# The last norm of a hybrid convolution layer: means taken from two places, powers without a Newton step, a spread in quarters

## The chip, the cores and the metric

The kernel runs on one NeuronCore of a Trainium2 chip. The metric is the device time of one execution in microseconds (us); smaller is better. A core has a matrix engine (TensorE, PE in the profile), a vector engine (VectorE, DVE), a scalar engine (ScalarE, ACT), a general engine (GpSimd, POOL) and a queue engine (SyncE, SP). Each works through its own instructions in order, and they wait for one another by semaphores. Transfers between HBM and the on-chip memory SBUF are issued here from SP and from ACT. PSUM is the memory into which TensorE writes; VectorE and ScalarE can read it.

## The reference, cut to what matters

One layer: a short gated convolution, then a SwiGLU feed-forward part, each between two RMS norms, with shift, scale and gate from a conditioning vector. There are 2048 tokens of 1024 features, in float32.

```python
def rms_norm(x, g):
    xf = x.astype(jnp.float32)
    y = xf * lax.rsqrt(jnp.mean(xf * xf, axis=-1, keepdims=True) + RMS_EPS)
    return (y * g.astype(jnp.float32)).astype(x.dtype)

mod = c_act @ ada_w[i] + ada_b[i]
sh_m, sc_m, g_m, sh_f, sc_f, g_f = jnp.split(mod, N_ADA, axis=-1)
h = modulate(rms_norm(x, norm_gains[i, 0]), sh_m, sc_m)
h = short_conv_mixer(h, conv_w_in[j], conv_w[j], conv_w_out[j])
x = x + g_m[:, None, :] * rms_norm(h, norm_gains[i, 1])
h = modulate(rms_norm(x, norm_gains[i, 2]), sh_f, sc_f)
h = swiglu(h, ffn_w_gate_up[i], ffn_w_down[i])
x = x + g_f[:, None, :] * rms_norm(h, norm_gains[i, 3])
```

The last line is what the end of the kernel computes for its last 512 tokens.

## The kernel before

**Tiles and stages.** Features lie on the 128 partitions and tokens along the free axis, in tiles of 128 x 512, so that a vector of 1024 features is eight tiles (`KD = 8`). The tokens are worked in two halves of 1024 (`NU = 2`), and each of these in two groups of 512 (`tok` 0 and 1). Four matrix products follow one another for each half: `in`, `out`, `gu` and `down`; the stages run in the order in0, out0, in1, out1, gu0, down0, gu1, down1. Each product is worked with seven products of blocks instead of eight (P1 to P7), and each of these with operands split into a high and a low part in a shorter float format (three passes in place of a float32 one).

**The order of the work.** The program is written out by hand, slot by slot. A slot is one product of blocks on TensorE. `later(n, f)` puts a step `n` slots behind the present one, and `due()` runs what has come due, once ahead of a slot's product and once behind it (the half slots). All engines take their instructions in the order in which the program is written.

**A norm.** The squares of eight tiles are added up in one tile (`add_square`: the square by ACT, the add by GpSimd, or by VectorE for some tiles of the last stage). `norm_of_sums` takes the mean over the partitions: for each 128 tokens, a product with the sum's columns as stationary operand and a column of 1/1024, so that 128 means lie in one column of a PSUM bank. `root` (line 218) raises mean + eps to the power -1/2 on GpSimd, and then does a Newton step in three operations on VectorE, whose result is the power times -2; line 158 multiplies the gains by -0.5 to make up for it. `diagonal` puts the four columns of 128 factors on the diagonals of four 128 x 128 blocks, and `spread` multiplies them by a matrix of ones, so that each of the 512 tokens has its factor on all partitions. `root` is used in sixteen places: twice in the start (lines 1111 and 1260, names r0 and r1), for the rows of the second half (r2, r3), behind each `out` stage (n.., m..), behind each `down` stage (o..), and in `last_half`.

**The start.** `vt` holds the small vectors (biases, gains, taps, conditioning), loaded by ACT's queue. VectorE sets some constants, waits for `vt` to scale the gains (line 158), and then fills `w` with ones (line 1200), with which `warm(8)` runs passes on TensorE that compute nothing used. The first factor is worked from the squares of the rows in `factor(0)`, spread, and multiplied into the first features.

**The last stage.** In down1 the slots are sorted so that the tiles of the second token group become ready one after another (line 511). The tiles are `down1z`; when one is ready, `ready_z` (line 649) has its square taken and added (`down1q`), and the tile scaled by gain and gate on ACT. The eighth has a square of its own (`ph.sq`, in the profile `lastq`). Then `last_half` (line 1011) runs:

- for five tiles (`ON_PE`), x times the identity is put into a PSUM bank (`lastx`) ahead of time, two before the means and three behind them;
- the means of the sum of seven squares and of the eighth square, eight products of one column each for both (`lasts`);
- eps and the sum of the two (`lastv`), power (`lastp`), Newton step (`lastt`, and `lastq` again), diagonal (`lastd`), spread (`lastb`, one product over 512 columns);
- for each tile, VectorE multiplies z by the spread in PSUM. For the five of `ON_PE` TensorE adds z to x in `lastx`, ACT copies the bank and issues the output; for the other three VectorE adds x and SP issues the output.

A float32 product takes two passes on TensorE in the profile. Every operation is recorded on line 78, that of the helper `Engine`, so the profile's rows are told apart by the names of tiles.

Of the kernel before, what the change touches and what calls it, by code (L numbers as in the profile page):

```python
# [10 lines left out]
F32 = mybir.dt.float32  # L11
F32R = mybir.dt.float32r
AF = mybir.ActivationFunctionType
ALU = mybir.AluOpType

P = 128
# [3 lines left out]
KD = D // P  # L20
NF = FF // P
FH = NF // 2
EPS = 1e-6
CH = 512
# [13 lines left out]
VB, VG, VW, VC = 0, 48, 80, 104  # L38
# [11 lines left out]
def hybrid_conv_layer(  # L50
# [31 lines left out]
    V, A, PE, G, SP = map(Engine, (nc.vector, nc.scalar, nc.tensor, nc.gpsimd, nc.sync))  # L82
# [4 lines left out]
    bigs, pairs, raws, sb = (ctx.enter_context(tc.tile_pool(name=n, bufs=1)) for n in ("bigs", "pairs", "raws", "sb"))  # L87
# [12 lines left out]
    def tmp(name):  # L100
        return sb.tile([P, CH + 2], F32, tag="tmp", bufs=NTMP, name=name)

    def small(n, name):
        return sb.tile([P, n], F32, tag="small", bufs=16, name=name)

    def bank(name):
        return ps.tile([P, CH], F32, tag="mm", bufs=8, name=name)
# [5 lines left out]
    def later(slots, f):  # L113
        waiting.append((now[0] + slots, len(waiting), f))
# [26 lines left out]
    vt = const.tile([P, 112 + 24], F32, name="vt")[:, :112]  # L141
    A.dma_start(vt, vec)
    ident = const.tile([P, P], F32, name="ident")
# [4 lines left out]
    one = const.tile([P, P], F32, name="one")  # L148
    V.memset(one, 1.0)
    mean = const.tile([P, 1], F32, name="mean")  # L150
    V.memset(mean, 1.0 / D)
    mhalf = const.tile([P, 4], F32, name="mhalf")
# [2 lines left out]
    V.memset(carry, 0.0)  # L155
    cact = const.tile([P, KD], F32, name="cact")
    A.activation(cact, vt[:, VC : VC + KD], AF.Silu)
    V.tensor_scalar(vt[:, VG : VG + 4 * KD], vt[:, VG : VG + 4 * KD], -0.5, None, ALU.mult)
    mA = [const.tile([P, KD], F32, name=f"mA{i}") for i in range(2)]
    mB = [const.tile([P, KD], F32, name=f"mB{i}") for i in range(2)]  # L160
    mG = [const.tile([P, KD], F32, name=f"mG{i}") for i in range(2)]
# [1 line left out]
    def col(t, k):  # L163
        return t[:, k : k + 1]
# [52 lines left out]

    def root(v, name):

        p, t = small(4, name + "p"), small(4, name + "t")  # L220
        G.tensor_tensor(p, v, mhalf, ALU.pow)
        yield 1
        q = sb.tile([P, 4], F32, tag="q", bufs=8, name=name + "q")
        V.tensor_tensor(t, p, p, ALU.mult)
        V.tensor_tensor(t, t, v, ALU.mult)
        V.scalar_tensor_tensor(q, t, -3.0, p, ALU.add, ALU.mult)
        return q

    def at_once(gen):
        while True:  # L230
            try:
                next(gen)
            except StopIteration as e:
                return e.value

    def diagonal(q, name):
        dg = tmp(name + "d")
        for t in range(4):
            V.tensor_scalar(dg[:, t * P : (t + 1) * P], ident, q[:, t : t + 1], None, ALU.mult)
        return dg  # L240
# [13 lines left out]
    def norm_of_sums(acc, name):  # L254

        st = bank(name + "s")
        for t in range(4):
            PE.matmul(st[:, t : t + 1], acc[:, t * P : (t + 1) * P], mean, start=True, stop=True)
        v = small(4, name + "v")
        V.tensor_scalar(v, st[:, :4], EPS, None, ALU.add)  # L260
        yield 1
        return (yield from root(v, name))

    def norm_of_rows(g, name, put):
        s = [small(4, f"{name}a{i}") for i in range(2)]
        rows = [(t, i) for t in range(4) for i in range(2)]
        xr = {}

        def load(k):
            if k < len(rows):  # L270
                t, i = rows[k]
                xr[k] = raw(f"xr{g}{t}{i}")
                r0 = g * CH + t * P
                SP.dma_start(xr[k], x[r0 : r0 + P, i * CH : (i + 1) * CH])

        load(0)
        yield 2
        for k, (t, i) in enumerate(rows):
            load(k + 1)
            yield 2  # L280
            A.activation(xr[k], xr[k], AF.Square, scale=1.0 / 32.0, accum_out=s[i][:, t : t + 1])
        yield 1
        v = small(4, name + "v")
        V.tensor_tensor(v, s[0], s[1], ALU.add)
        V.tensor_scalar(v, v, EPS, None, ALU.add)
        yield 1
        q = yield from root(v, name)
        yield 1
        yield from spread_later(q, name, put, 6)
# [224 lines left out]
    class Group:  # L514
# [134 lines left out]
        def ready_z(self, c):  # L649
            ph = self.ph  # L650
            tok, n = {"11": (0, self.i), "12": (0, self.i + 4), "21": (1, self.i), "22": (1, self.i + 4)}[c]
            z = ph.z(tok, n)
            if c == "12":
                A.copy(z, self.pa)
            ph.tiles_done[tok] += 1
            scaled_z = partial(A.activation, z, z, AF.Copy, scale=col(mG[1], n))
            if ph.last and ph.tiles_done[1] == KD:
                ph.sq = tmp("lastq")
                A.activation(ph.sq[:, :CH], z, AF.Square)
                scaled_z()  # L660
            else:
                add_square(ph.acc, tok, z, f"{ph.name}q{tok}{n}", V if ph.last and c == "21" else G, 0.5 if ph.last else 1)
                if ph.last and tok:
                    later(1, scaled_z)
            ph.tile_ready(tok, n, z)
            if ph.tiles_done[tok] == KD:
                ph.half_ready(tok)

    def add_square(acc, key, z, name, E=G, lag=1):
        if key not in acc:  # L670
            acc[key] = tmp(name)
            A.activation(acc[key][:, :CH], z, AF.Square)
        else:
            sq = tmp(name)
            A.activation(sq[:, :CH], z, AF.Square)
            later(lag, lambda: E.tensor_tensor(acc[key][:, :CH], acc[key][:, :CH], sq[:, :CH], ALU.add))
# [189 lines left out]
    slots, first, own = [], {}, {}  # L866
# [25 lines left out]
    for s in slots:  # L892
        ph = s.ph
# [4 lines left out]
        else:  # L898
            b = of.setdefault((ph.name, s.n), Blocks(ph.kind, s.grp))
# [69 lines left out]
    def after_down(ph, tok):  # L969
        u = ph.u  # L970
        rb = {}
        if ph.last and tok:
            yield 1
            yield from last_half(ph)
            return
# [30 lines left out]
    def out_tile(u, tok, k):  # L1006
        return out[u * 2 + tok, k // 4][:, (k % 4) * CH : (k % 4 + 1) * CH]

    ON_PE = (4, 5, 6, 7, 0)

    def last_half(ph):

        u, tok = ph.u, 1
        sums = {}

        def add_x(k):
            sums[k] = bank(f"lastx{k}")
            PE.matmul(sums[k], ident, ph.xt[k], start=True, stop=False, skip_group_check=True)

        st = bank("lasts")  # L1020
        for k in ON_PE[:2]:
            add_x(k)
        for i, sq in enumerate((ph.acc[tok], ph.sq)):
            for t in range(4):
                PE.matmul(col(st, 4 * i + t), sq[:, t * P : (t + 1) * P], mean, start=True, stop=True)
        for k in ON_PE[2:]:
            add_x(k)
        v = small(4, "lastv")
        V.tensor_scalar(v, st[:, :4], EPS, None, ALU.add)
        V.tensor_tensor(v, v, st[:, 4:8], ALU.add)  # L1030
        dg = diagonal(at_once(root(v, "last")), "last")
        b = bank("lastb")
        PE.matmul(b, one, dg[:, :CH], start=True, stop=True)
        for k in ON_PE + tuple(k for k in range(KD) if k not in ON_PE):
            z, xt = ph.z(tok, k), ph.xt[k]
            V.tensor_tensor(z, z, b, ALU.mult)
            if k in ON_PE:
                PE.matmul(sums[k], ident, z, start=False, stop=True, skip_group_check=True)
                A.copy(xt, sums[k])
                A.dma_start(out_tile(u, tok, k), xt)  # L1040
            else:
                V.tensor_tensor(xt, xt, z, ALU.add)
                SP.dma_start(out_tile(u, tok, k), xt)
        yield

# [438 lines left out]
```

## Time and profile before

| what | us |
|---|---|
| median of 3 runs | 1970.31 (1970.17 to 1972.41) |
| the profiled execution, its own time | 1969.02 |
| its span in the profile | 1967.2 |
| TensorE busy in the span | 1939.6 |
| VectorE busy | 1464.8 |
| bytes moved | 459.51 MB, mean 234 GB/s |

The profile is of one execution. Times in rows count from the span's start. A row of the timeline reads: start, duration, engine, operation, what it writes <- what it reads, their shapes, how many alike were merged, and in brackets the idle time of the engine before it with what ended it. PEld is the weight load of TensorE, which overlaps the products; SPq and ACTq are the instructions by which SP and ACT issue transfers. A row of the windows reads: the window, its length, then for PE, PEld, DVE, ACT and POOL the busy time and the instructions, the granted clock of TensorE, the busy share of the transfer engines and GB/s. A row of GpSimd is rough.

### The profile page before, as it was taken

How to read it: one execution, taken by the hardware profiler on the slowest of the kernel's cores; microseconds unless marked ns; L12 is line 12 of the kernel's file. 1: busy time of each engine (PE TensorE's matmuls, PEld its weight loads, DVE VectorE, ACT ScalarE, POOL GpSimd, SP SyncE). 2: the span in 40 equal slices, each digit the busy share in tenths (PEclk: the TensorE clock that was granted, in tenths of full speed). 3: DMA queues.
4: the chain of work that ended last, by engine and by line, in shares of the span. 5: the costliest groups of instructions: out<-in, count | busy, mean ns of one | idle time of the engine just before them, and what ended most of it. 6: DMA issues, size and time to landing. Idle time of an engine off the chain costs nothing.

```text
span 1967.2 us, 24986 instructions
## 1 busy us (share of the span) xinstructions
PE 1939.6 (99%) x8468; PEld 1571.7 (80%) x8468; DVE 1464.8 (74%) x2159; ACT 870.2 (44%) x1430; POOL 342.4 (17%) x224
## 2 busy tenths in 40 slices
PE   8899999999999999999999999999999999999998
PEld 4578887777888888888888888888888888888886
DVE  5998888988998876997776755586776655665466
ACT  4533447534335643444333454463333333444452
POOL 0012202201221301243341410120100100111010
PEclk9999999999999999999999999999999999999999
DMA  9369859869996764677665977577554342386534
GB/s 390 137 230 390 306 178 350 314 236 373 327 319 228 265 228 146 223 240 249 212 211 189 307 292 264 181 278 270 195 194 136 126 142 97 118 312 232 196 133 133
DMA packets 204752, 459.51 MB, mean 234 GB/s; under 512 B 22864, under 2 KB 38352, under 8 KB 198224
## 3 DMA queue, kind: packets, MB, share of 16 engines
q1 hardware_dynamic: 180000, 403.52, 59.4%
q10 hardware_dynamic: 24624, 54.40, 7.2%
q8 instruction: 66, 1.08, 0.2%
q14 instruction: 62, 0.51, 0.1%
HBM read 326.75 MB, written 131.07 MB: 233 GB/s over the span
## 4 chain that ended last, share of the span: by engine, by line
PE 88%; DVE 5%; DMA 3%; issue 2%; ACT 1%; SPq 0%; POOL 0%; ACTq 0%; POOLq 0%; DVEq 0%
PE gu0P L78 21%; PE gu1P L78 21%; PE in0P L78 11%; PE down0P L78 11%; PE down1P L78 9%; PE in1P L78 8%; PE out1P L78 4%; PE out0P L78 2%; DVE in1c L78 0%; DVE ada L78 0%; DMA in0a<-xt_d 0%; DMA c<-c_row_d 0%; DMA y1S<-in1b1s 0%; DVE in1y L78 0%; PE pms L78 0%
## 5 line engine op out<-in xcount | busy, mean ns | idle before, releaser
L78 DVE TENSOR_TENSOR gu1a<-gu1P,gu1a 128x512 f32<-128x512 f32 x63 | 43.5, 691 | 108.6 <-PE gu1P L78 108.6
L78 DVE TENSOR_TENSOR gu0a<-gu0P,gu0a 128x512 f32<-128x512 f32 x63 | 43.3, 688 | 70.2 <-PE gu0P L78 68.6
L78 POOL TENSOR_TENSOR gu1a<-gu1a 128x512 f32<-128x512 f32 x11 | 19.0, 1726 | 363.5 <-DVE gu1g11s L78 42.5
L78 ACT COPY gu1a<-gu1P 128x512 f32<-128x512 f32 x42 | 24.7, 587 | 98.6 <-PE gu1P L78 87.4
L78 POOL TENSOR_TENSOR nq<-nq,nq 128x512 f32<-128x512 f32 x28 | 41.6, 1485 | 129.4 <-ACT nq L78 99.4
L78 ACT COPY gu0a<-gu0P 128x512 f32<-128x512 f32 x42 | 24.4, 586 | 83.8 <-PE gu0P L78 82.7
L78 DVE CUSTOM_DVE_ANT_0 ada<-ada,c 128x512 f32<-128x512 f32 x80 | 57.8, 733 | 0.0
L78 ACT COPY gu1g<-gu1P 128x512 f32<-128x512 f32 x24 | 14.1, 588 | 92.9 <-PE gu1P L78 92.9
L78 POOL TENSOR_TENSOR gu0a<-gu0a 128x512 f32<-128x512 f32 x11 | 19.4, 1767 | 171.4 <-ACT gu0a L78 48.0
L78 POOL TENSOR_TENSOR down0q<-down0q,down0q 128x512 f32<-128x512 f32 x14 | 23.8, 1703 | 144.1 <-ACT down0q L78 144.1
L78 ACT COPY gu0g<-gu0P 128x512 f32<-128x512 f32 x24 | 14.1, 587 | 75.9 <-PE gu0P L78 75.4
L78 POOL TENSOR_TENSOR down1q<-down1q,down1q 128x512 f32<-128x512 f32 x10 | 16.1, 1612 | 148.6 <-ACT down1q L78 148.6
L78 DVE TENSOR_TENSOR gu1g<-gu1P,gu1g 128x512 f32<-128x512 f32 x24 | 16.6, 691 | 27.4 <-ACT gu1g L78 26.0
L78 ACT ACTIVATE gu1a<-gu1a 128x512 f32<-128x512 f32 x42 | 26.6, 633 | 13.2 <-DVE xo L78 6.0
L78 DVE TENSOR_TENSOR down2P<-down2P,down2P 128x512 fp32r<-128x512 f32 x14 | 11.1, 794 | 28.6 <-ACT down2P L78 28.6
L78 ACT ACTIVATE gu0a<-gu0a 128x512 f32<-128x512 f32 x42 | 26.6, 633 | 11.7 <-DVE gu0a L78 10.4
L78 POOL TENSOR_TENSOR out1q<-out1q,out1q 128x512 f32<-128x512 f32 x14 | 22.3, 1594 | 51.2 <-ACT out1q L78 51.1
L78 POOL TENSOR_TENSOR out0q<-out0q,out0q 128x512 f32<-128x512 f32 x14 | 23.0, 1641 | 44.6 <-ACT out0q L78 44.5
L78 DVE TENSOR_TENSOR xx<-xx,zz 128x512 f32<-128x512 f32 x32 | 27.1, 847 | 1.1
L78 ACT ACTIVATE nq<-xx 128x512 f32<-128x512 f32 x32 | 20.2, 631 | 17.3 <-DVE xx L78 17.3
L78 DVE TENSOR_TENSOR gu0g<-gu0P,gu0g 128x512 f32<-128x512 f32 x24 | 16.5, 689 | 14.7 <-ACT gu0g L78 13.3
L78 DVE TENSOR_TENSOR down10P<-down10P,down10P 128x384 fp32r<-128x384 f32 x14 | 8.6, 615 | 22.3 <-ACT down10P L78 22.3
(3225 smaller groups left out, 6729.3 us busy)
## 6 DMA issues: line engine op xcount, KB each, us to landing
ada<-ada_d SPq DMA_DIRECT2D x64, 256.0 KB, 5.6
act0A<-gu0a SPq DMA_DIRECT2D x33, 256.0 KB, 3.5
act1A<-gu1a SPq DMA_DIRECT2D x33, 256.0 KB, 2.8
ada<-ada_d SPq DMA_DIRECT2D x16, 512.0 KB, 9.4
zz<-z SPq DMA_DIRECT2D x32, 256.0 KB, 5.2
xx<-xt_d SPq DMA_DIRECT2D x32, 256.0 KB, 5.5
x<-xx ACTq DMA_DIRECT2D x32, 256.0 KB, 4.9
down0S<-act0S SPq DMA_DIRECT2D x8, 1024.0 KB, 7.1
```

What stands on the lines that cost most here:

```text
L78: return tc.keep_in_program_order(f(*args, **kwargs))
```

## The change

1. `root` returns GpSimd's power itself. The three operations on VectorE behind it are gone in all sixteen places, and so is the scaling of the gains in the start.
2. The means of the first seven squares of the last token group are taken by `all_but_one`, 1.5 slots behind the slot in which the seventh tile becomes ready, between two products of the down stage; its bank is taken there too. In `last_half` eps is added to these ahead of the rest, and only the means of the eighth square are taken there.
3. The diagonal of the last norm is built block by block, and each block is spread by a product of its own over 128 columns.
4. Behind the spread, two products read the diagonal into a bank (`lastw`) that nothing reads.
5. TensorE adds x for four tiles instead of five, GpSimd for two (1 and 2), VectorE for two (0 and 3), and the tiles are taken in the order 0, 4, 1, 5, 6, 2, 7, 3 instead of 4, 5, 6, 7, 0, 1, 2, 3.

```diff
-    V.tensor_scalar(vt[:, VG : VG + 4 * KD], vt[:, VG : VG + 4 * KD], -0.5, None, ALU.mult)
...
     def root(v, name):
-        p, t = small(4, name + "p"), small(4, name + "t")
-        G.tensor_tensor(p, v, mhalf, ALU.pow)
+        q = sb.tile([P, 4], F32, tag="q", bufs=8, name=name + "q")
+        G.tensor_tensor(q, v, mhalf, ALU.pow)
         yield 1
-        q = sb.tile([P, 4], F32, tag="q", bufs=8, name=name + "q")
-        V.tensor_tensor(t, p, p, ALU.mult)
-        V.tensor_tensor(t, t, v, ALU.mult)
-        V.scalar_tensor_tensor(q, t, -3.0, p, ALU.add, ALU.mult)
         return q
...
                 if ph.last and tok:
                     later(1, scaled_z)
+                    if ph.tiles_done[1] == KD - 1:
+                        later(1.5, partial(all_but_one, ph))
...
-    ON_PE = (4, 5, 6, 7, 0)
+    ON_PE, ON_POOL, LAST_TURN = (4, 5, 6, 7), (1, 2), (0, 4, 1, 5, 6, 2, 7, 3)
+
+    def sums_of_squares(ph, sq, first):
+        for t in range(4):
+            PE.matmul(col(ph.st, t + 4 * first), sq[:, t * P : (t + 1) * P], mean, start=True, stop=True)
+
+    def all_but_one(ph):
+        ph.st = bank("lasts")
+        sums_of_squares(ph, ph.acc[1], True)
...
-        st = bank("lasts")
+        v = small(4, "lastv")
+        V.tensor_scalar(v, ph.st[:, 4:8], EPS, None, ALU.add)
         for k in ON_PE[:2]:
             add_x(k)
-        for i, sq in enumerate((ph.acc[tok], ph.sq)):
-            for t in range(4):
-                PE.matmul(col(st, 4 * i + t), sq[:, t * P : (t + 1) * P], mean, start=True, stop=True)
+        sums_of_squares(ph, ph.sq, False)
         for k in ON_PE[2:]:
             add_x(k)
-        v = small(4, "lastv")
-        V.tensor_scalar(v, st[:, :4], EPS, None, ALU.add)
-        V.tensor_tensor(v, v, st[:, 4:8], ALU.add)
-        dg = diagonal(at_once(root(v, "last")), "last")
-        b = bank("lastb")
-        PE.matmul(b, one, dg[:, :CH], start=True, stop=True)
-        for k in ON_PE + tuple(k for k in range(KD) if k not in ON_PE):
+        V.tensor_tensor(v, v, ph.st[:, :4], ALU.add)
+        q = at_once(root(v, "last"))
+        dg = tmp("lastd")
+        b, warm = bank("lastb"), bank("lastw")
+        for t in range(4):
+            c = slice(t * P, (t + 1) * P)
+            V.tensor_scalar(dg[:, c], ident, q[:, t : t + 1], None, ALU.mult)
+            PE.matmul(b[:, c], one, dg[:, c], start=True, stop=True)
+        for _ in range(2):
+            PE.matmul(warm, one, dg[:, :CH], start=True, stop=True)
+        for k in LAST_TURN:
             z, xt = ph.z(tok, k), ph.xt[k]
             V.tensor_tensor(z, z, b, ALU.mult)
...
-                V.tensor_tensor(xt, xt, z, ALU.add)
+                (G if k in ON_POOL else V).tensor_tensor(xt, xt, z, ALU.add)
                 SP.dma_start(out_tile(u, tok, k), xt)
```

## Prediction

> **What bounds the kernel now.** I read the page's busy shares first, then busy time by windows, and then the timeline of the two ends and of every place where TensorE waits.
>
> ```profile
> PE 1939.6 (99%) x8468; PEld 1571.7 (80%) x8468; DVE 1464.8 (74%) x2159; ACT 870.2 (44%) x1430; POOL 342.4 (17%) x224
> ```
> ```profile
> 460.00:1940.00 1480.00, 1479.81 (x6543) 1222.02 (x6542) 1070.03 (x1483) 640.83 (x1036) 270.02 (x173) 1.00 0.64 221
> ```
>
> TensorE is busy 1939.6 of 1967.2 us, and from 460 to 1940 us it idles 0.19 us. Nothing that VectorE or GpSimd do less of in there can be seen. The change can act on the last 27 us, on the first 60, and on the few waits before 460; its reach is the 27.6 us in which TensorE idles, plus what it does for itself at the end.
>
> The end, from the last product of the down stage on (start, duration, engine, operation):
>
> ```profile
> 1947.47 0.69 DVE L78 TENSOR_TENSOR down1z<-down1P,down1z 128x512 f32<-128x512 f32 x1 [4.81 <-PE down1P L78]
> ...
> 1948.25 0.63 ACT L78 ACTIVATE lastq<-down1z 128x512 f32<-128x512 f32 x1 [6.10 <-DVE down1z L78]
> ...
> 1948.98 0.95 PE L78 MATMUL lasts<-mean,down1q 128*128 128x1 f32 x8
> ...
> 1949.76 0.97 PEld L78 LDWEIGHTS lasts<-mean,lastq 128*128 128x128 f32 x8
> ...
> 1950.86 0.16 DVE L78 TENSOR_SCALAR lastv<-lasts 128x4 f32<-128x4 f32 x1 [2.70 <-PE lasts L78]
> 1951.06 0.16 DVE L78 TENSOR_TENSOR lastv<-lastv,lasts 128x4 f32<-128x4 f32 x1
> ...
> 1951.30 1.02 POOL L78 TENSOR_TENSOR lastp<-lastv,mhalf 128x4 f32<-128x4 f32 x1 [29.01 <-DVE lastv L78]
> ...
> 1952.94 0.88 DVE L78 TENSOR_SCALAR lastd<-ident,lastq 128x128 f32<-128x128 f32 x4
> ...
> 1953.87 1.12 PE L78 MATMUL lastb<-lastd,one 128*128 128x512 f32 x2 [0.36 <-DVE lastd L78]
> 1955.04 3.68 DVE L78 TENSOR_TENSOR down1z<-down1z,lastb 128x512 f32<-128x512 f32 x6 [1.22 <-PE lastb L78]
> ...
> 1956.94 0.58 ACT L78 COPY xl<-lastx 128x512 f32<-128x512 f32 x1 [7.30 <-PE lastx L78]
> ...
> 1959.47 2.98 SPq L78 DMA_DIRECT2D out_d<-xl  x3
> ...
> 1961.40 0.69 DVE L78 TENSOR_TENSOR xl<-xl,down1z 128x512 f32<-128x512 f32 x1
> 1961.54 0.34 ACTq L78 DMA_DIRECT2D out_d<-xl  x1
> ```
>
> It is one chain: sum, square, means, power, Newton step, diagonal, spread, eight multiplies with three adds on VectorE, output. Every link shortened counts, until the eight output transfers stand in a row.
>
> **The end, part by part.** The means of the first seven tiles move into the stream of products, ahead of the weight load at 1942.28, and want a sum that VectorE ends at 1942.65:
>
> ```profile
> 1941.97 0.68 DVE L78 TENSOR_TENSOR down1q<-down1q,down1q 128x512 f32<-128x512 f32 x1
> ...
> 1942.28 0.41 PEld L78 LDWEIGHTS down1P<-down1A221h,down7P 128*128 128x128 f32 x2
> ```
>
> TensorE would wait about 0.4 us there (1942.65 and 0.04 of signal, less 1942.28), with the rest of the down stage queued behind it; eight passes at 0.97 us for eight loads, less overlap, are 0.9. So the last product comes **1.3 us later**, and with it the sum (1948.8) and the square (ends 1950.25). Against that, the eight passes of the square no longer queue behind the other eight: they begin when the square is there, 1950.3, not at 1949.76. Adding eps beforehand takes 0.2 off, so the sum of the means starts near 1951.4 (before 1951.06) and the power ends 1952.7 (before 1952.32). With the Newton step gone, the diagonal begins then, not 0.62 behind the power: 1952.7 against 1952.94. Taking the means sooner thus gives back most of what the missing step wins; **0.2 us** are left.
>
> The spread: now two passes of 512 columns start after the fourth diagonal and VectorE goes on 1.22 us after it. In quarters, three of four pairs of passes lie under the diagonals. No row has a pass of 128 by 128 columns: 0.11 us is the pitch of the one-column passes above, 0.23 that of the 256-column passes quoted below. Eight passes by the first end at 1954.1, by the second at 1955.0, both with 0.2 us of latency (the two passes' 1.12 less twice 0.45, the pitch of 512 columns by the 256-column row). A quarter of 0.45 is 0.11, so I take the near end and a little: multiplies from **1954.3**, 0.7 earlier.
>
> From there VectorE has ten operations instead of eleven (8 x 0.61, 2 x 0.61, three short drains: 6.4 us against 7.05), because two adds go to GpSimd. Do these hold VectorE up?
>
> ```profile
> 1915.78 1.48 POOL L78 TENSOR_TENSOR down1q<-down1q,down1q 128x512 f32<-128x512 f32 x1 [19.53 <-ACT down1q L78]
> ...
> 1916.14 1.67 DVE L78 TENSOR_TENSOR xo<-xo,down1z 128x512 f32<-128x512 f32 x1
> ```
> ```profile
> 868.83 2.66 POOL L78 TENSOR_TENSOR down0b<-down0b,down0b 128x512 f32<-128x512 f32 x2
> ```
> ```profile
> 870.05 0.68 DVE L78 TENSOR_TENSOR gu0a<-gu0P,gu0a 128x512 f32<-128x512 f32 x1
> ```
>
> An add with both operands in SBUF waits until GpSimd is done (1.67 instead of 0.69); one that reads PSUM does not (0.68 inside GpSimd's 2.66). The multiplies read the spread from PSUM, so only the last add may wait, some 0.1 us. Issues of the outputs, from the first multiply: on SP, in this order, tile 0 at 1.4, GpSimd's two at 4.1 and 5.9 (1.48 each), tile 3 behind them at 6.4; ACT's four at 3.8, 5.1, 6.1 and 7.0, by 1.84 from multiply to issue (1956.94 + 0.62 - 1955.72, the end of the first multiply) and the copies' pitch of 1.0 us ((1961.54 - 0.62 - 1956.94)/4). The last issue is ACT's now, at 1961.3, against SP's last at 1962.1: 0.8 earlier. But four transfers of 256 KB are then issued within 1.1 us:
>
> ```profile
> 1960.40:1965.00 4.60, 0.00 (x0) 0.00 (x0) 1.66 (x3) 0.70 (x2) 0.00 (x0) 1.00 1.05 330
> 1965.00:1966.00 1.00, 0.00 (x0) 0.00 (x0) 0.00 (x0) 0.00 (x0) 0.00 (x0) 0.77 0.08 31
> ```
>
> The transfers already run without a gap until 1965, at 0.8 us each (256 KB at 330 GB/s). The tighter pack gives back 0.3: the end gains **0.5 us**. The idle passes on the diagonal cost nothing, since they end (4 x 0.45) before the first product that adds a tile; nor do they win anything, as the granted clock is 1.00 here already. Bounds of the end: +0.2 (quarters at the dear end) and -1.3 (multiplies at 1954.1, no packing).
>
> **The Newton steps elsewhere.** Sixteen powers lose three small operations on VectorE, 0.16 to 0.2 us each. Only three stand where something waits.
>
> ```profile
> 50.97 0.16 DVE L78 TENSOR_TENSOR r1t<-r1p 128x4 f32<-128x4 f32 x1
> ...
> 51.44 0.69 DVE L78 TENSOR_TENSOR in0A12l<-in0b,in0A12h 128x512 fp32r<-128x512 f32 x1
> ```
> ```profile
> 53.60 1.10 PE L78 MATMUL r1b<-r1d,one 128*128 128x512 f32 x2 [0.66 <-DVE r1d L78]
> ```
>
> At 51 us VectorE has no gap, and TensorE waits 0.66 us for its diagonal: the whole **0.47 us** (51.44 - 50.97) is won and is carried on.
>
> ```profile
> 306.77 1.25 DVE L78 TENSOR_TENSOR r3t<-r3p 128x4 f32<-128x4 f32 x1
> ```
> ```profile
> 314.26 0.74 PE L78 MATMUL out0P<-out0S10h,out0P 128*128 128x512 f32 x2 [1.61 <-ACT out0z L78]
> ```
>
> At 306.77 the first of the three, with both operands in SBUF, takes 1.25 us instead of 0.16, like the add above; behind it stands the sum whose copy TensorE awaits 1.61 us. Between 0 and 1.61 can be won; transfers are dense there, so I take **0.5**.
>
> ```profile
> 374.08 0.15 DVE L78 TENSOR_TENSOR n00t<-n00p 128x4 f32<-128x4 f32 x1
> ```
> ```profile
> 381.56 0.74 PE L78 MATMUL in1P<-in1S3h,in4P7k 128*128 128x512 f32 x2 [0.23 <-DVE in1c L78]
> ...
> 390.40 0.50 PE L78 MATMUL in1P<-in1S2l,in3P6k 128*128 128x512 f32 x1 [0.57 <-DVE in1S2l L78]
> ```
>
> At 374 VectorE works without a gap and TensorE waits for it 0.23 and 0.57 us shortly after: again **0.47** of these 0.80.
>
> **The start.** Scaling the gains goes, and it waited for a load:
>
> ```profile
> 4.86 0.18 DVE L78 TENSOR_SCALAR vt<-vt 128x32 f32<-128x32 f32 x1 [3.82 <-DMA vt<-vec_d]
> 5.09 0.48 DVE L78 MEMSET w<- 128x512 f32 x1
> ```
> ```profile
> 5.63 9.14 PE L78 MATMUL wb<-w,one 128*128 128x512 f32 x16 [5.63 <-DVE w L78]
> 14.72 1.12 PE L78 MATMUL r0b<-r0d,one 128*128 128x512 f32 x2
> 15.78 3.61 PE L78 MATMUL pms<-ada,cact 128*1 128x256 f32 x16
> ```
> ```profile
> 18.27 1.90 DVE L78 TENSOR_TENSOR in0a<-in0a,r0r 128x512 f32<-128x512 f32 x3 [1.15 <-DMA in0a<-xt_d]
> ```
>
> The first factor comes 0.6 sooner, but the multiply it feeds waits 1.15 us for its load at 18.27 anyway: **0**. Less obvious is that the warm-up passes now start near 1.6 us instead of 5.63 and end near 10.7, which leaves TensorE idle some 3.4 us ahead of r0b at 14.1. At the end of the run the clock stays at 1.00 from the last pass at 1960.3 until the 0.77 of 1965 to 1966 (half rate from about 1965.5, 5.2 us later), so 3.4 us should not cost the clock. [...]
>
> **Sum.** -0.5 (end) - 0.47 - 0.5 - 0.47 = -1.9 us. The profiled execution took 1969.02 us (span 1967.2), so 1967.1; the median shown is 1970.31, 1.3 above it, and the forecast against that is **1968.4**.
>
> **Rivals.**
> 1. The clock falls in the new gap. The 16 pms passes, 3.61 us at full rate, and what follows run at half rate until the clock is back. At 0.45 the 16 warm-up passes would take 7.2 us; the 9.14 are 1.9 more, so four of them ran at twice the time, and the clock is up after some 4 us: from r0b at 14.1 to 18.1 the passes since 15.2 would lose 1.4, less 0.3 of slack; if it takes longer, up to the 3.6 of all passes, less 0.2. That is **1.1 to 3.4 us** on the chain. For it: 3.4 us of new idle; against: the 5.2. It outweighs the gains from 1.9 up. At 3.2: 1971.6, **slower than before**. Chance 0.15.
> 2. The end wins nothing, so that the means are not taken sooner in effect: quarters at 0.45 us, the multiplies at 1955.0, outputs packed (+0.2), and the gains at 306 and 374 lost to loads (-0.47 kept). 1970.0. For it: the 1.3 us put into the stream. Chance 0.16.
> 3. All waits go: 1.61 at 314, 0.80 at 381 to 390, 0.47, and 1.3 at the end, -4.2: 1966.1. For it: those rows are idle time of TensorE. Against: transfers next in line. Chance 0.14.
>
> **How the numbers follow.** The forecast has 0.52; 0.03 is left for what I don't see. A measurement tells about 0.2% from no change, 3.9 us: faster than 1966.4 or slower than 1974.2. Rival 3 lies at the border, most of it beyond: 0.12 faster. Only a longer half-rate stretch or the unseen reaches 1974: 0.03. The range goes from below rival 3, 1965.7, to rival 1, 1971.7.
>
> **What would show it.** After: a TensorE wait of 0.4 us on the seven-tile sum inside the down stage, and the stream's last product 1.3 us later against the one before the sums; diagonals 0.4 us or less behind the power; quarters done within 0.7 us of the last diagonal; no multiply above 0.7 us; r1b 0.47 sooner against the load; warm-up from 1.6 us, and pms passes at 0.23 each. Passes at 0.45 there, or multiplies at 1.6 beside GpSimd, would make me wrong, and so would a wait before 460 us that grows.

## The result and the profile after

| kernel | median us (runs) | lowest to highest | ratio, 95% interval | profiled execution, span |
|---|---|---|---|---|
| before | 1971.01 (22) | 1968.90 to 1972.41 | | 1969.02, 1967.2 |
| after | 1968.51 (22) | 1965.70 to 1971.11 | 0.9987, 0.9981 to 0.9993 | 1968.34, 1966.5 |

The change wins 2.5 us of 1971, with 1.4 to 3.7 in the interval (0.0007 and 0.0019 of 1971): measured, and below the 3.9 us (0.2%) that the forecast gave as the least by which a time can be told from no change. The page of after, busy shares:

```profile
PE 1943.6 (99%) x8474; PEld 1573.7 (80%) x8474; DVE 1456.2 (74%) x2109; ACT 869.2 (44%) x1429; POOL 347.1 (18%) x226
```

TensorE is busy 4.0 us *longer* than before in a span that is 0.7 us shorter. Its new idle passes (1.88 us in `lastw`) stand against the passes of the tile that it no longer adds (`lastx` 9.26 us before, 7.95 after), so most of the 4.0 is work that ran slowly. The start in the timeline of TensorE, after (start, duration, engine, operation, wait):

```profile
1.64 9.93 PE L78 MATMUL wb<-w,one 128*128 128x512 f32 x16 [1.64 <-DVE w L78]
14.20 2.07 PE L78 MATMUL r0b<-r0d,one 128*128 128x512 f32 x2 [2.64 <-DVE r0d L78]
16.20 4.25 PE L78 MATMUL pms<-ada,cact 128*1 128x256 f32 x16
```

r0b takes 2.07 instead of 1.12. After, busy time by windows (the third figure from the right is the granted clock):

```profile
14.00:16.00 2.00, 1.80 (x2) 0.50 (x2) 2.00 (x8) 0.00 (x0) 0.00 (x0) 0.53 1.05 438
16.00:18.00 2.00, 2.00 (x7) 0.63 (x7) 0.59 (x2) 0.59 (x1) 0.00 (x0) 0.62 0.97 400
72.00:74.00 2.00, 1.78 (x5) 1.45 (x5) 2.00 (x5) 0.01 (x1) 0.00 (x0) 0.54 1.02 418
74.00:76.00 2.00, 2.00 (x7) 1.53 (x7) 2.00 (x5) 1.95 (x3) 0.00 (x0) 0.61 1.02 416
```

The granted clock fell twice: behind the new gap of 2.64 us, and again at 72 us, where before's profile has 1.00. The second fall follows a wait that both kernels have. The waits ahead of 460 us in the timeline of TensorE, after:

```profile
53.80 1.10 PE L78 MATMUL r1b<-r1d,one 128*128 128x512 f32 x2 [0.19 <-DVE r1d L78]
...
71.54 0.51 PE L78 MATMUL in0P<-in0S3h,in2P 128*128 128x512 f32 x1 [1.80 <-ACT in2P L78]
...
314.55 0.73 PE L78 MATMUL out0P<-out0S10h,out0P 128*128 128x512 f32 x2 [0.56 <-ACT out0z L78]
...
374.70 0.70 PE L78 MATMUL in1P<-in1A12h,in5P2k 128*128 128x512 f32 x2 [0.88 <-DMA in5P2k<-kin5P]
```

Two waits shrank, 0.66 to 0.19 at r1b and 1.61 to 0.56 at 314; at 374 TensorE waits for a load, which costs nothing in the end (see n00 below). The end in the timeline of after:

```profile
1940.19 0.69 DVE L78 TENSOR_TENSOR down1z<-down1P,down1z 128x512 f32<-128x512 f32 x1 [1.48 <-PE down1P L78]
...
1942.92 0.97 PEld L78 LDWEIGHTS lasts<-mean,down1q 128*128 128x128 f32 x8 [0.48 <-DVE down1q L78]
1943.81 0.30 PEld L78 LDWEIGHTS down1P<-down1A221h,down7P 128*128 128x128 f32 x2
...
1948.95 0.69 DVE L78 TENSOR_TENSOR down1z<-down1P,down1z 128x512 f32<-128x512 f32 x1 [6.08 <-PE down1P L78]
...
1950.41 0.97 PEld L78 LDWEIGHTS lasts<-mean,lastq 128*128 128x128 f32 x8 [0.62 <-ACT lastq L78]
...
1951.74 1.02 POOL L78 TENSOR_TENSOR lastq<-lastv,mhalf 128x4 f32<-128x4 f32 x1 [29.25 <-DVE lastv L78]
1952.80 0.88 DVE L78 TENSOR_SCALAR lastd<-ident,lastq 128x128 f32<-128x128 f32 x4 [1.13 <-POOL lastq L78]
1953.14 1.16 PE L78 MATMUL lastb<-lastd,one 128*128 128x128 f32 x8
1954.13 1.88 PE L78 MATMUL lastw<-lastd,one 128*128 128x512 f32 x4
1954.33 0.69 DVE L78 TENSOR_TENSOR down1z<-down1z,lastb 128x512 f32<-128x512 f32 x1 [0.66 <-PE lastb L78]
...
1955.66 4.27 DVE L78 TENSOR_TENSOR down1z<-down1z,lastb 128x512 f32<-128x512 f32 x7
```

To read the end apart from what lies ahead of it, I measure four stretches and their sum: from the sum of the tile before the last (1940.19 here, 1939.98 before) to the last tile's sum; from there to the first diagonal; to the first multiply by the spread; to the end of the span.

| profile | tile before to last sum | to first diagonal | to first multiply | to the end | all |
|---|---|---|---|---|---|
| before | 7.49 | 5.47 | 2.10 | 12.16 | 27.22 |
| after | 8.76 | 3.85 | 1.53 | 12.17 | 26.31 |

Spans are shown to a tenth of a microsecond, so the last two columns are good to about 0.05. The end wins **0.91 us**: 0.35 by the first two columns together, 0.57 by the spread, nothing after it.

### The profile page after: what moved, and what is told of

Same layout as the page of the kernel before. It is cut to its first block, busy times and chain, and to the rows that moved or that the text cites. A ratio compares the mean times of both kernels' runs of the same rounds, so it can differ in the third digit from the quotient of the medians.

```text
span 1966.5 us, 24967 instructions
## 1 busy us (share of the span) xinstructions
PE 1943.6 (99%) x8474; PEld 1573.7 (80%) x8474; DVE 1456.2 (74%) x2109; ACT 869.2 (44%) x1429; POOL 347.1 (18%) x226
## 4 chain that ended last, share of the span: by engine, by line
PE 87%; DVE 5%; DMA 4%; ACT 2%; issue 1%; SPq 0%; POOL 0%; ACTq 0%; DVEq 0%
PE gu0P L78 21%; PE gu1P L78 21%; PE in0P L78 11%; PE down0P L78 11%; PE down1P L78 11%; PE in1P L78 5%; PE out1P L78 4%; PE out0P L78 2%; DMA x<-xx 1%; DMA kgu2P<-gu2P 1%; PE pms L78 1%; DVE in1c L78 0%; DVE in1y L78 0%; DMA xr<-x_d 0%; DVE ada L78 0%
```

## The experiments

**Theory.** The win comes from the two waits ahead of 460 us and from the end; it is diminished by clock falls, one of which the change invites by its earlier warm-up. **Rivals**: the falls or the waits are absorbed by later loads; the end's parts win otherwise than in the sum above (sharing, idle passes, the early means). All kernels were timed in five rounds against before, in three groups on one chip each (before: 1971.36 us with experiments 1 to 4, 1970.94 with 5, 6, 7 and 9, 1970.74 with 8 and 10 to 12).

**1. The end alone**: after, with before's roots and scaling (the last norm keeps its raw power; its diagonals multiply by -2 to match the gains).

```diff
...
-            V.tensor_scalar(dg[:, c], ident, q[:, t : t + 1], None, ALU.mult)
+            V.tensor_scalar(dg[:, c], ident, q[:, t : t + 1], -2.0, ALU.mult, ALU.mult)
```

> The new end alone; the other fifteen powers keep their Newton step and the gains their scaling, and the last diagonal takes the factor -2. Theory A (each part has a gain of its own, and the start of the changed kernel gives some back through a fallen clock): warm-up from 5.6 us as before, r0b 1.1 us and the pms passes 3.6 us; the sum of the last tile some 1.3 us later than before, the span's end 0.9 us nearer to it beyond these 1.3; time 0.9 us under before, ratio 0.9995. Theory B (the end wins nothing, all comes from the powers): ratio 1.0000 or above, the end as far behind the last sum as before (19.7 us).

**2. The roots alone**: before, with the raw power in all sixteen places and no scaling.

```diff
...
-        V.tensor_tensor(t, p, p, ALU.mult)
-        V.tensor_tensor(t, t, v, ALU.mult)
-        V.scalar_tensor_tensor(q, t, -3.0, p, ALU.add, ALU.mult)
```

> The end of before, with raw powers in all sixteen places and no scaling of the gains. Theory A: TensorE's wait at 314 us shrinks from 1.6 to some 0.6 us, r1b's from 0.66 to 0.2; warm-up from 1.6 us with a gap of 2.6 us ahead of r0b; where the clock falls in it, r0b takes 2.1 us and all to 300 us lies 0.7 us later or more, elsewhere not; 1.6 us under before, ratio 0.9992, plus 0.6 at the end itself, 0.9989. Theory B as to the powers (their gains are lost to transfers): ratio 0.9997 or above.

The end alone: 1970.12 us, 0.9991 (0.9982 to 1.0000). The roots alone: 1969.41, 0.9985 (0.9976 to 0.9994). From last sum to the end the first has after's 17.56 us. The second has 5.47 - 4.88 = 0.59 won by the missing Newton step alone, and TensorE's waits at r1b and 314 are 0.19 and 0.56 us in it, as in after: the powers' gains there are not lost. Neither part carries the whole by its time; the intervals overlap. The clock speaks more clearly: the roots alone, with a gap of 3.58 us ahead of r0b, lost it at 14 to 18 us; the end alone, without the gap, did not, but both lost it at 72.

**3. and 4. No gap at the start, two ways**: eleven warm-up passes instead of eight, or the warm-up held back behind an operation that reads `vt`.

```diff
-        warm(8)
+        warm(11)
```
```diff
+        late = small(4, "late")
+        V.tensor_scalar(late, vt[:, VG : VG + 4], -0.5, None, ALU.mult)
         V.memset(w, 1.0)
```

> The changed kernel with 22 warm-up passes instead of 16, which fill the gap ahead of r0b. Theory A (the clock falls because TensorE idles 2.6 us): r0b 1.1 us, pms 3.6 us, clock 1.00 from 12 to 20 us, the first waits of TensorE behind them 0.7 us sooner than in the changed kernel's profile; time 0 to 0.7 us under the changed kernel's 1968.5. Rival (the fall is not tied to the gap): r0b again 2.1 us.

> The changed kernel with one small operation ahead of the fill of w that waits for the vectors' load, as the scaling did before, so that the warm-up starts at 5.6 us again. Theory A: no gap, r0b 1.1 us, pms 3.6 us, as with 22 passes; time within 0.3 us of that kernel. Rival: the clock falls here too.

1967.82 (0.9983, 0.9974 to 0.9992) and 1968.17 (0.9985, 0.9977 to 0.9994): no fall at 14 to 18 us in either, and the second waiting product of in0S2l comes at 84.35 and 84.34 instead of 84.92: 0.6 us won there. In the median 0.7 and 0.3, within the intervals. Both still fell at 72.

**5. The means late again**: the seven-tile means behind the first two additions of x, not in the stream.

```diff
-                    if ph.tiles_done[1] == KD - 1:
-                        later(1.5, partial(all_but_one, ph))
...
-        V.tensor_scalar(v, ph.st[:, 4:8], EPS, None, ALU.add)
         for k in ON_PE[:2]:
             add_x(k)
+        all_but_one(ph)
+        V.tensor_scalar(v, ph.st[:, 4:8], EPS, None, ALU.add)
         sums_of_squares(ph, ph.sq, False)
```

> The changed kernel with the means of the seven tiles back behind the last product (eps is still added ahead). Theory A (taking them inside the stream costs a wait and eight passes ahead of the last sum, and gives less back): the last sum comes 1.3 us sooner than in the changed kernel, the power starts 0.4 us sooner by the same clock and start, and the end gains 0.4 us. Rival (the means taken sooner do win): the power starts later by up to 0.9 us.

1969.12 us, 0.9991 (0.9982 to 1.0000); last sum to diagonal 5.16, to the first multiply 3.10, to the end 12.07. The 5.16 is 1.31 more than in after, so already up to the diagonal this order takes as long as after (7.49 + 5.16 = 12.65, after 12.61) and gives none of the 0.4 us that were expected. Of this 5.16, 0.28 are more than the roots alone have (4.88): the square's means go into the bank from which VectorE first takes the seven tiles' means.

```profile
1949.68 1.02 PE L78 MATMUL lasts<-mean,lastq 128*128 128x1 f32 x8 [0.35 <-DVE lastv L78]
```

The 3.10 was not expected either. Busy time by windows of this kernel:

```profile
1948.50:1950.50 2.00, 1.65 (x17) 1.60 (x15) 0.16 (x1) 0.54 (x1) 0.00 (x0) 1.00 0.00 0
1950.00:1951.50 1.50, 1.50 (x9) 1.03 (x9) 0.16 (x1) 0.00 (x0) 0.52 (x1) 0.93 0.00 0
1951.50:1953.50 2.00, 2.00 (x4) 0.75 (x3) 0.87 (x4) 0.00 (x0) 0.50 (x1) 0.50 0.00 0
```

The clock fell at about 1951.3, with TensorE idle for only 0.35 us in the first of these windows; what had run there were sixteen passes of one column. The half rate lay on two additions of x and on the spread and cost 3.10 - 1.53 = 1.57 us, more than the 1.27 that the stream saved. Whether late means are better in another place is left to experiment 12.

**6. One spread** over 512 columns instead of quarters.

```diff
-            PE.matmul(b[:, c], one, dg[:, c], start=True, stop=True)
+        PE.matmul(b, one, dg[:, :CH], start=True, stop=True)
```

> The changed kernel with the spread in one product over 512 columns behind the four diagonals. Theory A: first multiply 2.10 us behind the start of the first diagonal, as before, instead of 1.53; end 0.5 us later. Rival (quarters are bound by their weight loads and win nothing): 1.6 us or less.

1969.32 us, 0.9989 (0.9980 to 0.9998). From diagonal to multiply 2.10, as before, and last sum to the end 18.03 instead of 17.55: the quarters are worth 0.5 to 0.6 us.

**7. The old sharing** of the eight last adds, idle passes kept.

```diff
-    ON_PE, ON_POOL, LAST_TURN = (4, 5, 6, 7), (1, 2), (0, 4, 1, 5, 6, 2, 7, 3)
+    ON_PE, ON_POOL, LAST_TURN = (4, 5, 6, 7, 0), (), (4, 5, 6, 7, 0, 1, 2, 3)
```

> The changed kernel with five adds on TensorE, none on GpSimd and the old order of tiles. Theory A (the outputs stand in a row, so the shorter work of VectorE only packs them closer): from the first multiply to the end of the span 12.2 us, as in the changed kernel and before; no change in time. Rival (the sharing wins what VectorE saves): 12.9 us, 0.7 us slower.

1969.58 us, 0.9993 (0.9984 to 1.0002), and the whole end 27.52 us instead of 26.31. From first diagonal (1953.95) to first multiply 2.29, not 1.53. Its timeline of TensorE:

```profile
1952.49 2.82 PE L78 MATMUL lastx<-xl,ident 128*128 128x512 f32 x6
1955.14 1.05 PE L78 MATMUL lastb<-lastd,one 128*128 128x128 f32 x8
```

With a fifth tile, the products that put x into the banks hold TensorE until 1955.31, and the quarters begin 1.19 us behind the first diagonal, in after 0.34 (1953.14 - 1952.80). From first multiply to the end 12.66, half a microsecond more than after's 12.17. But the roots alone, with the same old sharing and no idle passes, have 12.20. The 12.66 is thus not the sharing's: here the first multiplied tile is one that TensorE adds, and its product stands behind the idle passes (ACT's first copy comes 2.57 us behind the first multiply, before 1.90). Behind the first multiply sharing wins nothing on its own; it makes room for the idle passes. Ahead of it, it makes room for the quarters, which is worth 0.76 here (2.29 - 1.53).

**8. No idle passes**: after without them.

```diff
-        for _ in range(2):
-            PE.matmul(warm, one, dg[:, :CH], start=True, stop=True)
```

> The kernel after without the two idle passes that read the diagonal. Theory that they win and cost nothing: 1.53 from first diagonal to first multiply, 12.2 from first multiply to the end, granted clock 1.00 until 1960, time as after (1968.5). Rival that they hold the clock up: the windows between the quarters and the first added tile show less than 1.00, and the products that add a tile take over 1 us, 13 us to the end. Rival that they delay: the first added tile's product 0.4 us sooner and 11.8 to the end.

1968.99 us, 0.9990 (0.9981 to 0.9998). The end has 1.54 and 12.14, as after. Its windows there:

```profile
1954.00:1956.00 2.00, 0.92 (x8) 0.73 (x7) 1.30 (x4) 0.00 (x0) 0.00 (x0) 1.00 0.00 0
1956.00:1958.00 2.00, 0.98 (x2) 0.30 (x2) 2.00 (x4) 0.00 (x0) 0.36 (x1) 1.00 0.34 131
1958.00:1960.00 2.00, 1.93 (x5) 0.67 (x4) 2.00 (x5) 1.17 (x2) 1.48 (x2) 1.00 0.19 75
```

The clock stays at 1.00 with TensorE idle half of four microseconds. In this profile the idle passes neither win nor cost. Since the wait of 1.8 us at 70, in which TensorE is idle without a break, lost the clock in only 7 of 11 profiles, one profile doesn't show that it never happens here. The mean clocks of the timed runs leave it open too: 10 of these 11 runs have 0.997 or less, of after's 22 only 10. The idle passes may thus keep a fall away in some executions; in which part of the run the clock was lost isn't on record.

**9. The means a slot later** in the stream.

```diff
-                        later(1.5, partial(all_but_one, ph))
+                        later(2.5, partial(all_but_one, ph))
```

> The changed kernel with the seven tiles' means one product later (2.5 slots instead of 1.5), when their sum has long been ready. Theory A: TensorE's wait of 0.48 us on that sum goes, the last sum and all behind it come 0.48 us sooner. Rival (the wait is taken up behind it): no change from the last sum's time on.

1968.51 us, 0.9985 (0.9976 to 0.9993). The timeline of this kernel:

```profile
1938.43 0.69 DVE L78 TENSOR_TENSOR down1z<-down1P,down1z 128x512 f32<-128x512 f32 x1 [0.27 <-PE down1P L78]
...
1946.86 0.69 DVE L78 TENSOR_TENSOR down1z<-down1P,down1z 128x512 f32<-128x512 f32 x1 [5.74 <-PE down1P L78]
```

8.43 us from tile to tile instead of 8.76: the 0.48 us wait was the order's (0.33 of it is won). The time doesn't resolve so little. This profile shows no fall anywhere, and is the cleanest measure of the roots: TensorE is 2.24 us ahead of before at the last wait ahead of 460 (432.59 against 434.83). At 463 it waits 0.85 us for a load, in6P3k, and keeps 1.57 (461.82 against 463.39).

**10. Both gaps filled**: eleven warm-up passes, and eight idle products of 128 columns (sixteen passes) in the wait at 70 us, into the bank that a later product takes anyway.

```diff
-        warm(8)
+        warm(11)
...
+        pre[12] = bank(f"{s.ph.name}{s.op}_{s.n}")
+        for _ in range(8):
+            PE.matmul(pre[12][:, :P], one, one, start=True, stop=True)
...
```

> The kernel after, with eleven warm-up passes instead of eight, so that TensorE has no gap ahead of r0b, and with eight idle passes of 128 columns in the wait at 70 us. Theory that the granted clock falls in either gap in part of the executions (0.6 and 1.4 us at the second multiply of in0S2l, 83 us): no half-rate window at 72, that multiply at 82.9 us or sooner, and, where transfers don't set 314 and 374, about 1 us less than the kernel after: 1967.4. Rival that the transfers at 314 and 374 us absorb what is won before: 83 us looks as expected, but 314 stays at 313.3 or later and the time at 1968.5. Rival that the idle passes themselves delay the real ones: a TensorE wait of over 1.8 us around 70.

**1966.24 us**, 0.9979 (0.9970 to 0.9987). Its timeline of TensorE, and one window:

```profile
68.81 1.95 PE L78 MATMUL in0P<-one 128*128 128x128 f32 x16
70.76 0.50 PE L78 MATMUL in0P<-in0S3h,in2P 128*128 128x512 f32 x1
```
```profile
72.00:74.00 2.00, 2.00 (x10) 1.63 (x10) 2.00 (x5) 0.72 (x2) 0.00 (x0) 1.00 1.02 416
```

No fall, the waiting product of in0S2l at 82.93 instead of 84.92, and 314 at 312.55 instead of 314.55: all 2.0 us are still there at 314, so the rival that loads absorb it falls there. At 461.76 TensorE then waits 1.09 us for in6P3k, and 1.56 us are left at the tile before the last (1938.63 against 1940.19). The interval overlaps with after's; the highest of 11 runs is 1968.27, below the median of after.

**11. Both gaps filled, means a slot later.**

> Both gaps filled and the seven-tile means one step later in the stream. Theory that TensorE's 0.48 us wait for the sum is the order's alone: no wait on that sum, the last sum 8.4 us behind the tile before it, the end as after (17.55): 0.35 less than with both gaps filled alone. Rival that it moves to another wait: the last sum 8.8 behind.

1966.21 us, 0.9978 (0.9969 to 0.9987): from tile to tile 8.42, 0.34 less than in experiment 10, as expected; the time can't tell it.

**12. Both gaps filled, and another end**: the means of seven tiles right behind the last product, one addition, the square's means, two additions, quarters, the fourth addition in the place of the idle passes.

```diff
+        all_but_one(ph)
         V.tensor_scalar(v, ph.st[:, 4:8], EPS, None, ALU.add)
-        for k in ON_PE[:2]:
-            add_x(k)
+        add_x(4)
         sums_of_squares(ph, ph.sq, False)
...
```

> The same start with both gaps filled, and another end: the seven-tile means are not in the stream but right after the last product, ahead of one tile's addition; the quarters stay; two tiles are added before the quarters and one, in the place of the idle passes, behind them. Theory that the early means cost what they win: no added time in the stream (the last sum 7.5 us behind the sum of the tile before it, not 8.8), square's sums 0.4 us later than after, so 4.25 from last sum to first diagonal, 1.53 from there to the first multiply, and 17.95 from the last sum to the end: 0.9 less than after; time 1966.6. Rival that the late means lose the clock at the end, as with the means late before: half-rate windows near the diagonals, 3.1 from diagonal to multiply, 19.5 to the end, and 1968.

**1964.96 us**, 0.9973 (0.9964 to 0.9983), the fastest of all: 1.3 us below experiment 10 in the same group, 3.5 below after by the medians (by the ratios to before 2.8; the intervals overlap from 0.9981 to 0.9983). From experiment 10 the intervals don't part it; the whole end is 25.06 us in its profile, against 26.17 there. Its timeline:

```profile
1939.74 0.69 DVE L78 TENSOR_TENSOR down1z<-down1P,down1z 128x512 f32<-128x512 f32 x1 [0.43 <-PE down1P L78]
...
1947.23 0.69 DVE L78 TENSOR_TENSOR down1z<-down1P,down1z 128x512 f32<-128x512 f32 x1 [4.81 <-PE down1P L78]
...
1951.08 0.88 DVE L78 TENSOR_SCALAR lastd<-ident,lastq 128x128 f32<-128x128 f32 x4 [1.14 <-POOL lastq L78]
1952.62 0.69 DVE L78 TENSOR_TENSOR down1z<-down1z,lastb 128x512 f32<-128x512 f32 x1 [0.66 <-PE lastb L78]
```
```profile
1947.03 0.95 PE L78 MATMUL lasts<-mean,down1q 128*128 128x1 f32 x8
1947.84 1.11 PE L78 MATMUL lastx<-xl,ident 128*128 128x512 f32 x2
1948.78 0.97 PE L78 MATMUL lasts<-mean,lastq 128*128 128x1 f32 x8
```

7.49 to the last sum, as before; 3.85 and 1.54 behind it, as after; 17.57 to the end: 0.4 better than I expected, since the square's means come 1.55 us behind the last sum (1948.78 - 1947.23), hardly later than in after (1950.46 - 1948.95 = 1.51). The late means cost nothing when they stand ahead of the additions. Even so, this profile lost the clock once, at a third place:

```profile
81.17 0.50 PE L78 MATMUL in0P<-in0S2l,in0P 128*128 128x512 f32 x1 [0.84 <-DVE in0S2l L78]
...
82.98 0.71 PE L78 MATMUL in0P<-in0S2l,in0P 128*128 128x512 f32 x1 [0.85 <-DVE in0S2l L78]
```
```profile
82.00:84.00 2.00, 1.15 (x4) 0.84 (x4) 2.00 (x4) 0.37 (x1) 0.00 (x0) 0.77 0.00 0
84.00:86.00 2.00, 2.00 (x6) 1.56 (x5) 1.97 (x5) 1.00 (x2) 0.00 (x0) 0.50 0.00 0
```

**All profiles together.** A fall is a 2 us window below 1.00.

| stretch | kernels | falls |
|---|---|---|
| 14 to 18 us, gap of 2.6 to 3.6 us ahead of r0b | after, 2, 5, 6, 7, 8, 9 | 4 of 7 (after, 2, 7, 8) |
| 14 to 18 us, gap of 1.3 us or none | before, 1, 3, 4, 10, 11, 12 | 0 of 7 |
| 70 to 80 us, wait of 1.8 us open | before, after, 1 to 9 | 7 of 11 (after, 1, 2, 3, 4, 7, 8) |
| 70 to 80 us, wait filled | 10, 11, 12 | 0 of 3 |
| 82 to 90 us, two waits of 0.84 us | all 14 | 2 of 14 (7, 12) |
| 1948 to 1952 us, sixteen one-column passes in a row | before, 2, 5 | 1 of 3 (5) |

A fall costs 0.6 us at the start (84.92 - 84.35) and 1.4 at 72 (84.35 - 82.93). In experiment 8 both windows from 14 to 18 us have 0.50 (after 0.53 and 0.62), and the same product came at 86.33, 2.0 later than in experiment 3. The fall at 72 also came in experiment 1, which has before's roots and warm-up: it isn't the change's.

**When the clock fell.** In after's trace the half rate begins at 14.12, at 72.14 and, behind the last pass, at 1963.13 us; the first two times it lasts 3.41 us. In the other profiles the windows add up to 3.4 us for each fall ahead of the last pass, but for the one at the start of experiment 8, which lasted 4.0 us at least (14 to 18). How busy TensorE was just ahead of it does not tell by itself whether the clock falls: from 68.73 to 72.14 us TensorE was busy 1.52 of 3.41 us in after, which then lost the clock, and 1.39 in before, which kept it. The gap ahead of r0b was 2.64 us in after, with a fall, and 3.23 in experiment 5, where the windows from 12 to 20 us have 1.00. What decides it in one execution or another, these runs do not show.

**The clock of the timed runs.** Every timed run lists its mean granted clock. The profiles with no fall ahead of the last pass (before, 6, 9, 10, 11) have 0.999 or 1.000, and a fall of 3.41 us takes 0.0009 (half of 3.41 in 1967). At 0.998 or less were 50 of the 97 runs of before that were taken beside the experiments, 20 of after's 22, and none of the 22 of experiments 10 and 11. So about half of before's runs, at least, lose the clock somewhere inside, and its profile, 2.0 us below its median, is one that doesn't. The two runs of after with 0.999 took 1965.70 and 1966.40 us, as long as experiment 10.

## Why the prediction was right, and where its steps were off

The time came as forecast, 1968.51 against 1968.4, but that the two agree to 0.1 us is partly luck: several terms were off and made up for one another, and before's median over 22 runs was 0.7 above the 1970.31 that I started from. The gain is 2.5 us, not 1.9. The terms below add up to 2.94 in the profiles (0.91 at the end, 0.47, 1.05 and 0.51), and the start gives 0.16 beyond r1 (83.56 before, 82.93 in experiment 10, which has no fall), yet the two spans differ by only 0.7. After's two falls take back 2.0 (84.92 against 82.93 in experiment 10), where before's profile has none, and some 0.5 are lost in the unbroken products from 463 to 1940 us (1477.11 us against 1476.59), which nothing here explains. The medians are further apart because most of before's runs are slower than the one in its profile.

- **r1, -0.47**: right to the hundredth (0.66 to 0.19).
- **r3, -0.5**: mis-sized, it is 1.05 (1.61 to 0.56). On VectorE the sum behind the three operations came 1.57 us sooner against the subtraction ahead of them (305.09 to 308.33 before, 306.43 to 308.10 after); the rest of ACT's chain keeps 0.56. I chose a low value for fear of transfers; none stood there.
- **n00, -0.47**: right, 0.51: from the wait at 314 to that at 390 take 76.14 us before and 75.63 after. VectorE works there almost without a gap and sets the wait at 390. All 12 profiles without the Newton step have 75.25 to 75.69, and experiment 1, which keeps it, 76.24. The wait at 374 between them, which a load of in5P2k ends in after, is 0.31 to 1.77 us long in these 12 and takes nothing from the gain. "Transfers next in line", rival 3's counterweight, held only at 463, where a load took 0.67 of 2.24 us (experiment 9).
- **The means sooner**: the wait was 0.48 (0.4 forecast), the last product 1.27 later (1.3), and 0.35 left of the missing Newton step (0.2). Here the sign is worth a look: the missing step alone gives 0.59 (experiment 2), so taking the means sooner *loses* 0.24 against that order (against experiment 5's, with eps added between the two groups, it is even). Experiment 12 shows what it was after: the early means' 3.85 without the 1.27, by order alone.
- **The quarters**: forecast 0.5 net of the 0.2 above, measured 0.57; the passes run at the near end. It rests on a condition that the sum did not name: TensorE must be free when the first diagonal is there. With five tiles added by TensorE it isn't, and from diagonal to multiply takes 2.29 (experiment 7).
- **The outputs, +0.3 for the tighter pack**: wrong, first multiply to end is 12.17 against 12.16. VectorE is done 0.7 us sooner behind the first multiply, as forecast (1960.66 - 1954.33 against 7.05), but ACT's last issue stands at 1961.37, 7.04 behind it; before, SP's last issue followed VectorE's last add, which ended 7.05 behind it. So behind the first multiply the sharing wins nothing and the packing takes nothing; the 0.8 of the last issue were the multiplies' alone. The sum gave the end 0.5, and it is 0.91: rival 2 falls. GpSimd's adds slowed no multiply (0.61 us each in the row of seven), as forecast.
- **The idle passes, nothing**: right in the one profile without them (experiment 8); the mean clocks of its timed runs leave open whether they keep a fall away elsewhere.
- **The start, 0, "3.4 us should not cost the clock"**: the step that failed. I held one row of the run's end (half rate 5.2 us behind the last pass) against the new gap. In after's own end it takes 2.6 us (last pass ends 1960.52, half rate from 1963.13), and gaps of 2.6 to 3.6 us lost the clock in 4 of 7 profiles. One row of one execution could not tell what the next would do. Rival 1 had the fall; its price, 1.1 to 3.4, was too high for a fall of 3.4 us: pms wasn't on the chain throughout, and 0.6 us arrive at 84. The longer fall of experiment 8, with 2.0, lies inside it.

**Open**: why the clock falls in one execution and not in another. It fell behind the wait of 1.8 us in 7 of 11 profiles, behind the two waits of 0.84 us in 2 of 14, and in experiment 5 at about 1951.3 us, with TensorE busy 1.65 of 2 us from 1948.5 on, so idle time in the profile is not all that goes with a fall. How much of the 2.3 us from after to experiment 10 (1.6 by the ratios to before) is the 72 us fall and how much the start's isn't settled by times either; by the profiles 1.4 and 0.6 in the executions that have them.

## What to carry to other kernels

Before work is moved into a full stream to have it sooner, look at what it stands behind where it is: here an exchange of two groups on TensorE gave the same lead without 1.27 us in the stream. An operation that sits between a wait and its releaser on a full engine is worth as much as that wait allows, so read the wait, not the operation's own time. Before an order of small products is changed, ask what else stands on the engine when they are due: the quarters won 0.57 us only because TensorE had one tile less to add. And where the matrix engine pauses for two or three microseconds (here 1.8 to 3.6 us, with a fall behind 11 of 18 such pauses), fill the pause with idle passes and check the clock by windows, in the mean clock of many runs too, since one profile shows one execution: two such fills were worth 2.3 us by the medians of two groups of runs, the rebuilt end of the change 0.9 by its profile, that of experiment 12 2.2 (27.22 - 25.06).

## What the runs showed of the hardware

The granted clock fell to half behind gaps of 2.6 to 3.6 us ahead of r0b (4 of 7 profiles), behind the wait of 1.8 us at 70 (7 of 11) and behind two waits of 0.84 us (2 of 14), and once in a stretch of one-column passes with only 0.35 us of idle time (experiment 5). It lasted 3.41 us in after's trace (from 14.12 and from 72.14), 3.4 by the windows of the other profiles, and once 4.0 at least (experiment 8). Passes of 128 by 128 columns in float32 take 0.12 us each (1.95 for sixteen); filling the wait of 1.8 us with sixteen of them delayed nothing: the product behind it begins at 70.76, 0.05 behind ACT's cast (70.10 + 0.61), the same 0.05 as in after (71.54 against 70.88 + 0.61).
